# First tile in two transfers of one queue, memory tokens issued later, and new engine orders in a two-layer decoder kernel

## Chip, core and metric

The kernel runs on one core of a Trainium2 chip. The core has five engines that run side by side, each through its own list of instructions: TensorE (matmuls), VectorE, ScalarE, GpSimd and SyncE, which here only issues transfers. They wait for one another by semaphores. Data is moved by 16 DMA engines; SyncE, ScalarE and GpSimd each have a queue on which they issue transfers. The metric is the device time of one launch in microseconds, as a median over several runs.

## The reference

A decoder trunk of two layers over 256 tokens of width 1024, in 32-bit floats. Layer 0 mixes tokens by a gated unit, layer 1 by causal attention; in both, a 4-head attention into 256 memory tokens runs beside the mixer. Each layer ends in a gated feed-forward block, and every sublayer in `LayerNorm(alpha*x + f(x))`.

```
h = x @ a_w_in                       # layer 0: u (768), v (768), q_mem (256)
u = gelu(u); v = layer_norm(gelu(v), ln_g, ln_b)
mix = u * (causal(w_s) @ v + b_s)    # in chunks of 128 positions
...
h = x @ b_w_in                       # layer 1: q, k, v, q_mem
mix = softmax(q k^T / 8, causal) @ v
...
mem_out = softmax(q_mem k_mem^T / 8) @ v_mem ;  k_mem, v_mem = mem @ w_mem_kv
x = layer_norm(alpha*x + concat(mix, mem_out) @ w_mix_out)
x = layer_norm(alpha*x + (silu(x @ w_g) * (x @ w_u)) @ w_ffn_out)
```

## The kernel before

**Split operands.** Every matrix is multiplied as a high and a low part. `split` (L378) makes them: ScalarE casts the 32-bit values to the matmul's format (L379, "CAST"), VectorE subtracts the cast from the original (L380, "TENSOR_TENSOR"). Of the four products of parts the three larger ones are computed, in the order of `LO_LAST`: high x high, low tokens x high weights, high tokens x low weights.

**The weight stream.** `Stream` (L194) loads weights in units of 128 x 2048 numbers (1 MB) into four raw buffers (`RAW_BUFS`) and splits them in halves into ten buffers (`HALF_BUFS`). A raw buffer is loaded anew when both its halves have been split. The units `qm0`, `u0` and `km0` come in two transfers each (`IN_HALVES`).

**The first product.** The loop at L426 computes `va`, the values of the gated unit, and fills the stream by hand. Eight tiles (kk = 0 to 7), two to a raw buffer `raw_v`, each hold 256 columns of transposed tokens and 768 columns of weights, 512 KB. For each tile the tokens' high part is cast (L439, by VectorE for the first three tiles, then by ScalarE), their low part made (L440), the weights are split, for the first two tiles in two cuts of 384 columns, and twelve matmuls of 384 columns are issued: six with the first 384 weight columns, then six with the rest. Tile 0 comes in three transfers (L436), the others in one each (L438).

**Warm-up.** 37 small matmuls on zeros (`WARM`, L415) are issued before the first product.

**What follows it** in layer 0: the memory queries (`hqm`, weights `qm0`), `pu` (weights `u0` to `u2`), the memory keys (`hkm`) and values (`pvm`), then the gating product `sv`, which needs the normalised values `vn` (scaled at L965 and L966) and the mask-multiplied `wsT`. The memory tokens come in four transfers of 256 KB (`mraw`, L920).

**The tail.** The last token tile's output is normalised in three pieces of 512, 384 and 128 columns (`LAST_PIECES`): subtract the mean and multiply by the gain (L511), multiply by the inverse deviation and add the bias (L512), store (L514). The inverse deviation comes from L507 on VectorE and L508 on GpSimd. The last piece is stored by ScalarE's queue, the others by SyncE's.

**Order.** TensorE runs in the order in which the code issues its matmuls (`manual_schedule`). For VectorE, ScalarE and SyncE a table gives the order: `keep_order` (L358) numbers an engine's instructions as the code emits them, from 0, and chains them in the order of the table. On VectorE, 0 and 1 are two small memsets (L410, L412), 2 and 3 the high and low part of tile 0's tokens, 4 and 5 the low part of the first and the second cut of its weights, 6 to 9 the same for tile 1. On ScalarE, 0 is a table load (L400), 1 the small transfer at L425, 2 the transfer of tile 0 at L436, 3 and 4 the casts of tile 0's two cuts. On SyncE, 0 and 1 are tile 0's two transfers, 2 to 8 the other tiles, 9 and 10 the halves of `qm0`, 11 and 12 those of `u0`, 13 and 14 `u1` and `u2`, 15 and 16 the halves of `km0`, 17 the gain row, 18 to 21 the memory tokens, 22 `wsT`.

Of the kernel before, what the change touches and what calls it, by code (L numbers as in the profile page):

```python
# [22 lines left out]
D = 1024  # L23
T = 256
# [169 lines left out]
class Stream:  # L194
# [128 lines left out]
)  # L323
SCALAR_ORDER = (
# [30 lines left out]
)  # L355


# [865 lines left out]
```

## Time and profile before

| what | value |
|---|---|
| median of 3 runs | 552.55 us (552.26 to 552.84) |
| profiled execution, first to last instruction | 550.8 us |
| mean granted TensorE clock | 0.996 |
| bytes read from HBM | 119.42 MB, 219 GB/s over the span |

The profile is one execution. A row of its timeline gives start, length, engine, line, operation, output and inputs, shapes, how many instructions were merged, and in brackets how long the engine had been idle and what ended that. An engine name with a q ("SPq") is the engine's sequencer, which issues transfers. A matmul's length in the profile is from its start to the end of its pipeline, so consecutive ones overlap; the spacing of their starts is what one costs. In a row of stretches, the counts in brackets behind an engine's busy time are instructions that run in the stretch, and the last three numbers are the granted clock, the DMA engines' busy share and GB/s. Outside the span lie 1.75 us between the profiled span and the median of the runs.

### The profile page before, as it was taken

The page shows a single profiled execution, that of the slowest core. Times are in us where ns is not written, and L with a number is a line of the kernel's source. Part 1 is how long each engine was busy: PE and PEld are TensorE (multiplying, and loading weights), DVE is VectorE, ACT ScalarE, POOL GpSimd, SP SyncE. Part 2 cuts the span into 40 slices and gives each one's busy share as a digit, 9 for nine tenths or more (in the row PEclk, how much of TensorE's full clock was granted, in tenths as well). Part 3 has the DMA queues.
Part 4 walks back from the last instruction along what each step waited for, and adds up shares of the span by engine and source line. Part 5 has one row for each costly group of instructions (what it writes and reads, how often), then busy time and mean ns, then how long its engine had stood idle before and what let it go on. Part 6 is the DMA issues. An engine that isn't in the chain of part 4 may idle for free.

```text
span 550.8 us, 7698 instructions
## 1 busy us (share of the span) xinstructions
PE 542.6 (99%) x2835; PEld 460.6 (84%) x2835; DVE 501.5 (91%) x707; ACT 374.5 (68%) x574; POOL 47.7 (9%) x59
## 2 busy tenths in 40 slices
PE   9999999999999999999999999999999999999994
PEld 8988878888888888888898888788888888888884
DVE  5799978999999999999989688589999999999997
ACT  5868759785858677683565667668768676876720
POOL 1012001020202020100000000111202020201000
PEclk9999999999999999999999999999999999999998
DMA  8997668479796988878539234513597698897622
GB/s 303 384 398 265 223 259 221 154 131 328 155 343 132 300 220 229 275 271 273 198 137 397 105 130 161 114 77 153 97 360 133 249 266 271 233 255 220 218 69 77
DMA packets 23718, 120.97 MB, mean 220 GB/s; under 512 B 2688, under 2 KB 4736, under 8 KB 13824
## 3 DMA queue, kind: packets, MB, share of 16 engines
q1 hardware_dynamic: 17344, 99.16, 47.8%
q0 software_dynamic: 5760, 20.97, 21.4%
q8 instruction: 22, 0.36, 0.3%
q10 hardware_dynamic: 576, 0.34, 0.3%
q14 instruction: 16, 0.13, 0.1%
HBM read 119.42 MB, written 1.05 MB: 219 GB/s over the span
## 4 chain that ended last, share of the span: by engine, by line
PE 98%; DMA 1%; DVE 1%; DVEq 0%; ACT 0%; issue 0%
PE fof L404 11%; PE Xf L404 10%; PE Xg L404 10%; PE fog L404 9%; PE Zg L404 7%; PE Zf L404 7%; PE qk L404 6%; PE opc L404 4%; PE opa L404 4%; PE va L404 3%; PE bv L404 3%; PE pu L404 3%; PE pvm L404 3%; PE hkm L404 2%; PE hqm L404 2%; PE pg L404 2%
## 5 line engine op out<-in xcount | busy, mean ns | idle before, releaser
L379 ACT CAST spl_s_M<-raw_s_T 128x1024 fp32r<-128x1024 f32 x80 | 82.4, 1052 | 22.9 <-DVE raw_s_T L259 18.0
L380 DVE TENSOR_TENSOR spl_s_M<-raw_s_T,spl_s_M 128x1024 fp32r<-128x1024 f32 x80 | 95.6, 1217 | 2.4 <-ACT spl_s_M L379 2.1
L380 DVE TENSOR_TENSOR spl_s_M<-raw_s,spl_s_M 128x1024 fp32r<-128x1024 f32 x60 | 71.7, 1217 | 3.2 <-ACT spl_s_M L379 3.1
L379 ACT CAST spl_s_M<-raw_s 128x1024 fp32r<-128x1024 f32 x60 | 61.0, 1050 | 17.5 <-DMA raw_s<-in_w 13.3
L404 PE MATMUL fof<-spl_w,htf 128*128 128x512 f32 x264 | 63.0, 390 | 0.0
L404 PEld LDWEIGHTS fof<-spl_w,htf 128*128 128x128 f32 x264 | 49.3, 188 | 10.2
L404 PE MATMUL fog<-spl_w,htg 128*128 128x512 f32 x228 | 54.2, 390 | 0.0
L380 DVE TENSOR_TENSOR spl_w<-raw_w,spl_w 128x1024 fp32r<-128x1024 f32 x44 | 53.2, 1215 | 0.1
L404 PEld LDWEIGHTS fog<-spl_w,htg 128*128 128x128 f32 x228 | 42.7, 188 | 8.8
L259 DVE TENSOR_TENSOR raw_s_T<-raw_s_T,raw_s 128x1024 f32<-128x1024 f32 x40 | 48.4, 1217 | 0.1
L379 ACT CAST spl_w<-raw_w 128x1024 fp32r<-128x1024 f32 x44 | 45.7, 1055 | 1.0 <-PE fof L404 1.0
L404 PE MATMUL qk<-x2T,spl_qk 128*128 128x512 f32 x192 | 36.0, 343 | 0.0
L220 POOL DMA_DIRECT2D raw_s<-in_w x20 | 17.1, 856 | 217.1 <-DVE spl_s_M L380 201.4
L404 PEld LDWEIGHTS qk<-x2T,spl_qk 128*128 128x128 f32 x192 | 29.4, 188 | 4.4
L404 PE MATMUL Xg<-spl_s_M,SgM 128*128 128x512 f32 x120 | 29.4, 394 | 0.0
L404 PE MATMUL Xf<-spl_s_M,SfM 128*128 128x512 f32 x120 | 29.3, 393 | 0.0
L404 PE MATMUL Zg<-spl_s_M,SgM 128*128 128x512 f32 x120 | 28.9, 390 | 0.0
L404 PE MATMUL Xf<-spl_s_M,x1T 128*128 128x512 f32 x120 | 28.9, 390 | 0.0
L404 PE MATMUL Zf<-spl_s_M,SfM 128*128 128x512 f32 x120 | 28.8, 389 | 0.0
L404 PE MATMUL Xg<-spl_s_M,x3T 128*128 128x512 f32 x120 | 28.8, 389 | 0.0
L404 PEld LDWEIGHTS Zg<-spl_s_M,SgM 128*128 128x128 f32 x120 | 22.5, 188 | 4.8 <-DVE SgM L380 0.2
L404 PEld LDWEIGHTS Xg<-spl_s_M,x3T 128*128 128x128 f32 x120 | 22.5, 188 | 4.7
(265 smaller groups left out, 1068.8 us busy)
## 6 DMA issues: line engine op xcount, KB each, us to landing
raw_w<-in_w SPq DMA_DIRECT2D x22, 1024.0 KB, 6.6
raw_s<-in_w SPq DMA_DIRECT2D x20, 1024.0 KB, 7.1
raw_s_T<-in_w SPq DMA_DIRECT2D x10, 1024.0 KB, 7.0
raw_s_T<-in_w POOLq DMA_DIRECT2D x20, 512.0 KB, 8.6
raw_s<-in_w POOLq DMA_DIRECT2D x20, 512.0 KB, 5.5
raw_o<-in_w SPq DMA_DIRECT2D x8, 1024.0 KB, 6.4
raw_qk<-in_w SPq DMA_DIRECT2D x6, 1024.0 KB, 4.8
raw_v<-in_w SPq DMA_DIRECT2D x7, 512.0 KB, 8.1
```

Of the source, the lines that this page charges most:

```text
L220: self.nc.gpsimd.dma_start(self.raw[name][:, sl], self.unit_ap(other)[:, sl], accum_op=ALU.add)
L259: self.nc.vector.tensor_add(raw, raw, self.raw[used[1]][:, sl])
L379: nc.scalar.copy(hi, src)
L380: nc.vector.tensor_sub(lo, src, hi.bitcast(F32))
L404: nc.tensor.matmul(o, lhsT, rhs, start=start, stop=stop, skip_group_check=on)
```

## The change

Tile 0 comes in two transfers, both issued by SyncE: tokens and the first cut of the weights (640 columns, 320 KB), then the second cut (384 columns, 192 KB). ScalarE issues none of them, so it has 536 instructions instead of 537, and numbers above 2 in its table fall by one: 2 and 3 are now the casts of tile 0's two cuts, 15 the cast of tile 7's tokens, 40 to 43 those of the memory tokens. The three order tables are replaced. SyncE now issues the first memory tokens (18) behind the first half of `qm0` (9), and the next two behind the first half of `u0`. In the excerpt the tables are cut to their first and last lines.

```diff
 VECTOR_ORDER = (
-    0, 2, 3, 4, 5, 6, 7, 8, 9, 10, 11, 12, 13, 14, 16, 15, 18, 17, 19, 20, 22, 21, 23, 24, 34, 29, 33, 25, 32, 38, 37,
-    30, 27, 31, 28, 41, 46, 35, 26, 45, 49, 55, 42, 57, 47, 59, 50, 40, 1, 56, 64, 36, 58, 39, 63, 48, 95, 97, 43, 61,
...
-    661, 666, 663, 670, 664, 662, 671, 672, 673, 674, 675, 681, 676, 679, 677, 682, 680, 678,
+    0, 5, 2, 3, 4, 6, 8, 7, 9, 10, 11, 12, 14, 15, 13, 17, 16, 19, 18, 20, 21, 22, 23, 24, 33, 34, 47, 29, 25, 31, 37,
+    1, 26, 41, 42, 38, 35, 49, 46, 55, 50, 30, 36, 32, 63, 59, 39, 61, 48, 40, 56, 64, 45, 60, 27, 95, 44, 28, 57, 62,
+    51, 96, 52, 97, 58, 53, 43, 100, 54, 66, 67, 70, 74, 78, 71, 79, 69, 75, 68, 80, 73, 72, 98, 65, 81, 83, 85, 99,
...
+    669, 664, 661, 670, 671, 666, 672, 662, 673, 674, 675, 676, 677, 679, 678, 680, 681, 682,
 )
 SCALAR_ORDER = (
-    2, 3, 4, 5, 6, 7, 8, 9, 11, 10, 13, 14, 12, 15, 16, 0, 17, 1, 18, 19, 26, 27, 22, 24, 25, 31, 20, 32, 23, 41, 21,
...
+    3, 2, 4, 5, 6, 7, 8, 9, 11, 10, 13, 12, 14, 16, 40, 0, 15, 41, 17, 18, 25, 42, 22, 26, 24, 23, 21, 19, 30, 31, 35,
...
 )
 SYNC_ORDER = (
-    0, 1, 2, 3, 4, 18, 5, 6, 7, 8, 10, 9, 11, 12, 13, 14, 15, 19, 20, 16, 17, 24, 22, 25, 21, 26, 27, 28, 29, 23, 31,
...
-    113, 112, 115, 114,
+    0, 1, 2, 3, 4, 5, 6, 7, 8, 9, 18, 11, 19, 20, 10, 12, 13, 14, 21, 15, 16, 17, 24, 25, 22, 26, 27, 28, 23, 38, 29,
...
+    114, 115,
 )
...
                 if kk == 0:
-                    for q, c0, c1 in ((nc.sync, 0, T), (nc.scalar, T, T + 384), (nc.sync, T + 384, D)):
-                        q.dma_start(rk[:, c0:c1], src[:, c0:c1])
+                    for c0, c1 in ((0, T + 384), (T + 384, D)):
+                        nc.sync.dma_start(rk[:, c0:c1], src[:, c0:c1])
                 else:
                     nc.sync.dma_start(rk, src)
```

101 rows, old and new, of tables (SCALAR_ORDER, SYNC_ORDER, VECTOR_ORDER) are left out of this document.

## The prediction

> **What bounds the kernel now.** I read the shares on the page first, then what TensorE waited for, then the chain of waits over the first 60 us, which runs from the first transfer into matmuls that never stop.
>
> ```profile
> PE 542.6 (99%) x2835; PEld 460.6 (84%) x2835; DVE 501.5 (91%) x707; ACT 374.5 (68%) x574; POOL 47.7 (9%) x59
> PE warmup L415 <- DVE warm L410: 1.1, 1, 1.1
> 0.80 3.92 DMA raw_v<-in_w
> 4.72 0.02 issue
> 4.75 0.52 ACT spl_v L379
> 5.27 0.04 issue
> 5.31 17.52 PE va L404 x96
> ```
>
> The second line is all that the waits view lists for PE over the whole span: one wait, at the very start. From 5.31 us on TensorE always has its next operand in time. So the span has three parts: the way to the first real matmul (5.31 us), a matmul stream that no engine holds up, and a tail after the last matmul. The order of the matmuls is fixed by hand and the change doesn't touch it. It can therefore win only in the first and the last part; in the middle it can only lose, by making TensorE wait where it doesn't now.
>
> The stream has one soft place, its beginning. Rows of the timeline, TensorE alone, each from a narrow stretch (start, length, instructions that run in the stretch):
>
> ```profile
> 1.06 4.13 PE L415 MATMUL warmup<-warm 128*128 128x128 bf16 x37 [1.06 <-DVE warm L410]
> 5.31 1.56 PE L404 MATMUL va<-spl_v,x0T 128*128 128x384 f32 x4
> 6.71 2.60 PE L404 MATMUL va<-spl_v,x0T 128*128 128x384 f32 x14
> 7.76 5.71 PE L404 MATMUL va<-spl_v,x0T 128*128 128x384 f32 x32
> ```
>
> Later on 32 matmuls take 5.71 us; less the 0.33 us by which the last runs out, that is 5.38/31 = 0.173 us each. The fifth matmul starts at 6.71 us, so the first four took 1.40 us, 0.35 each, twice as long. The 37 warm-up matmuls of 128 columns took 0.11 us each, which is 0.33 for 384 columns: also half rate. TensorE thus runs at half rate from 1.06 to about 6.6 us, 5.5 us, whatever it does. The first four matmuls lose 1.40 - 4 x 0.173 = 0.71 us by it. That matters below: a start that comes later falls partly into time that is now spent at half rate.
>
> **The change part by part.**
>
> *The transfers of the first tile.* Before, SyncE issues tokens (128 KB) and the second half of the weights (192 KB), ScalarE the first half (192 KB).
>
> ```profile
> 0.80 0.42 ACTq L436 DMA_DIRECT2D raw_v<-in_w  x1
> 0.81 0.85 SPq L436 DMA_DIRECT2D raw_v<-in_w  x2
> 1.24 0.42 SPq L436 DMA_DIRECT2D raw_v<-in_w  x1
> raw_v<-in_w ACTq DMA_DIRECT2D x1, 192.0 KB, 3.9
> raw_v<-in_w SPq DMA_DIRECT2D x1, 192.0 KB, 4.0
> raw_v<-in_w SPq DMA_DIRECT2D x1, 128.0 KB, 3.7
> 2.00:4.00 2.00, 2.00 (x21) 2.00 (x20) 0.00 (x0) 0.53 (x1) 0.06 (x1) 1.00 0.79 187
> 4.00:6.00 2.00, 1.88 (x14) 1.61 (x12) 1.43 (x4) 1.02 (x2) 0.00 (x0) 1.00 1.05 377
> ```
>
> Issue plus time to landing: tokens 0.81 + 3.7 = 4.5, first half 0.80 + 3.9 = 4.7, second half 1.24 + 4.0 = 5.24 us. After, SyncE still issues two transfers at 0.81 and 1.24, so nothing behind them on its queue moves; ScalarE saves one issue of 0.42 us while it has nothing to do until 4.75, worth nothing. The same 512 KB (0.524 MB) must come. The last two rows end in the bytes' rate: 187 GB/s from 2 to 4 us, 377 after. If the first tile had the engines to itself, 0.374 MB would be there at 4.0 and the other 0.150 MB 0.4 us later, at 4.4. At the other end nothing changes, 5.24. For the second transfer I take 4.9, a third of the way in from the unchanged row: one queue fewer is in the way, but the next tile's transfers still crowd in from behind. The first transfer, 320 KB, lands before it and decides nothing, for the following reason.
>
> *The tables.* Number n in a table is the nth instruction of that engine as the code emits them. On VectorE 2 and 3 make the first tokens' high and low part, 4 and 5 the low part of the first and of the second half of the weights. The old table begins 0, 2, 3, 4, 5; the new one 0, 5, 2, 3, 4. On ScalarE, with the transfer gone, 2 and 3 are the casts of the first and second half; the new table begins 3, 2. Both engines are thus told to do the **second half first**, whereas the first matmuls use tokens and the first half. VectorE may not cast the tokens before it has made the low part of the second half, which needs ScalarE's cast of it, which needs the second transfer. Durations:
>
> ```profile
> 4.52 0.29 DVE L439 CAST x0T<-raw_v 128x256 fp32r<-128x256 f32 x1 [3.52 <-DMA raw_v<-in_w]
> 4.85 0.43 DVE L440 TENSOR_TENSOR x0T<-raw_v,x0T 128x256 fp32r<-128x256 f32 x1
> 5.29 1.07 DVE L380 TENSOR_TENSOR spl_v<-raw_v,spl_v 128x384 fp32r<-128x384 f32 x2
> ```
>
> From a landing at 4.90: cast of the second half 4.93 to 5.45 (0.52); its low part 5.47 to 6.00 (half of 1.07); token cast 6.01 to 6.30; first matmul 6.34 instead of 5.31. Token low part 6.34 to 6.77 (matmuls three and four need it), low part of the first half 6.78 to 7.31 (matmul five). So matmul five starts at 7.34 instead of 6.71: **+0.63 us**, if the clock has risen by about 6.6 as in this trace. In an execution where it rises before 5.3, the old kernel has its fifth matmul at 5.31 + 4 x 0.173 = 6.00 and the loss is 1.34. The three runs shown lie 0.58 us apart (552.26 to 552.84), about the size of the 0.71 that the half rate costs here, so both kinds may be among them. I take +0.85. With the landing at 4.4 the loss is at least 0.13, at 5.24 up to 1.68.
>
> *Tiles two to eight and the memory tokens.* The first memory transfer (256 KB) stood between tiles four and five and now goes out behind the first half of the memory queries' weights.
>
> ```profile
> 3.12 0.66 SPq L920 DMA_DIRECT2D mraw<-in_memT  x1
> 14.00:22.00 8.00, 8.00 (x48) 8.00 (x48) 5.55 (x9) 6.52 (x10) 0.00 (x0) 1.00 1.04 412
> 22.67 5.71 PE L404 MATMUL hqm<-x0T,spl_qm 128*128 128x512 f32 x32
> L241 SPq DMA_DIRECT2D raw_u<-in_w x2: 327/379/431, 11.9 to 12.3; - x2
> DMA to landing us min/median/max: 8.7/9.2/9.7
> 19.41 2.00 ACT L379 CAST spl_qm<-raw_qm 128x1024 fp32r<-128x1024 f32 x2 [1.00 <-DMA raw_qm<-in_w]
> 20.49 2.36 DVE L380 TENSOR_TENSOR spl_qm<-raw_qm,spl_qm 128x1024 fp32r<-128x1024 f32 x2 [0.75 <-ACT spl_qm L379]
> 16.28 1.28 ACT L400 ACT_TABLE_LOAD   x1
> ```
>
> Tiles five to eight land 256 KB / 400 GB/s = 0.65 us earlier. TensorE needs 12 x 0.173 = 2.08 us a tile and waited for none of them, so that is worth nothing. In exchange three memory transfers stand before the second half of the query weights. That half becomes the transfer that ends after 6.25 MB in units of 1024 KB, the place that the second part of raw_u has now: issued 12.3, at most 9.7 to landing, 22.0 us. ScalarE's cast (half of 2.00) and VectorE's low part (half of 2.36) end at 24.2. The query product starts at 22.67 + 0.63 = 23.3 and reaches that half after 8 of its 32 matmuls, 1.4 us, at 24.7. Cover 0.5 us; beyond that each us of lateness costs one. On ScalarE the cast of the first memory tokens and the table load (L400) now stand ahead of the eighth tile's token cast. Those memory tokens end the first 4.75 units, 4.98 MB: by the byte rates near 16 us, say 17 with the landing. Two casts (at most 1.0 each) and 1.28 later, at 20.3, the tile's tokens are there; it starts at 23.3 - 2.1 = 21.2. Cover 0.9 us.
>
> *The rest of the tables.* Both engines stay at the same instructions, only permuted. The tightest place that I find is the scaling of the gated values (instruction 58), moved to place 64, where the old order has the row that starts at 52.54.
>
> ```profile
> 52.54 0.75 DVE L470 TENSOR_TENSOR kkm<-hkm,kkm 128x256 fp32r<-128x256 f32 x2
> 51.60 1.02 DVE L966 SCALAR_TENSOR_TENSOR vn<-vn,rsv,gv 128x768 f32<-128x768 f32 x1
> 53.27 0.98 PE L404 MATMUL sv<-wsT,vn 128*64 128x128 f32 x14
> ```
>
> It would end at 52.54 + 1.02 = 53.56; TensorE wants it at 53.27 + 0.63 = 53.90. Cost nothing, bounded above by one scaling, 1.0 us. In the tail:
>
> ```profile
> 544.77 0.35 DVE L511 SCALAR_TENSOR_TENSOR xres<-xres,mvg,gb1ffn 128x128 f32<-128x128 f32 x1
> 545.04 0.15 DVE L507 TENSOR_SCALAR rsg<-mvg 128x1 f32<-128x1 f32 x1
> 545.11 1.27 DVE L511 SCALAR_TENSOR_TENSOR xres<-xres,mvg,gb1ffn 128x384 f32<-128x384 f32 x2
> 545.27 0.85 POOL L508 TENSOR_TENSOR rsg<-rsg,mhalf 128x1 f32<-128x1 f32 x1 [7.93 <-DVE rsg L507]
> 546.30 1.53 DVE L512 SCALAR_TENSOR_TENSOR xres<-xres,rsg,gb1ffn 128x128 f32<-128x128 f32 x3
> out<-xres SPq DMA_DIRECT2D x2, 256.0 KB, 2.2
> out<-xres ACTq DMA_DIRECT2D x2, 64.0 KB, 1.6
> ```
>
> The last tile keeps its six normalising steps, but the widest is no longer the last: the narrow pair is. Now VectorE ends at 546.30 + 1.53 = 547.83 and the 256 KB store behind it lands 2.2 us on, at 550.0. After: the small L507 first (544.77 to 544.84), two wide subtractions 1.2, their two scalings 1.2 (GpSimd's 0.85 is done by then), the narrow pair one behind the other 0.7: 547.9, and a 64 KB store that lands 1.6 us on, 549.5 to 549.6. **-0.4 us.**
>
> Sum: +0.85 - 0.4 = +0.45. The profiled execution (550.8) would become 551.25. The median of the runs, 552.55, is 1.75 above that span; I carry the difference over: **553.0 us**.
>
> **The rivals.**
>
> *A, the clock.* Slower. Warm-up ends at 5.19 (1.06 + 4.13) and TensorE would then idle 1.15 us instead of 0.12, just before its rate doubles. If idle time keeps the half rate, every matmul behind it costs 0.33 instead of 0.173, 48% of the time lost. Merely set back by 1.15 us, the doubling costs about 0.4; begun anew at 6.34 and lasting 5.5 us again, 2.6. I take the middle, 1.5: 554.5. For it: the half rate ended long after a seemingly full stretch of work. Against: four fifths of the time stays busy. It decides only if the gap lies before the doubling.
>
> The Trainium skill, page "TensorE: Matmul & The Clock Gate", Part 1, says that the clock is released after a window of about 3.4 us sustained activity that runs free of the kernel's start. The 5.5 us here are one window and part of another, which agrees. An estimate by that page: a window spoilt by the gap costs one more window at half rate, 3.4 x 0.48 = 1.6 us.
>
> *B, an early pair.* With one queue both parts come together, at 4.0, sooner than the byte rate above allows. Then the first matmul starts at 5.44; the fifth has its data at 6.44, but four at half rate take until 6.84. The start loses 0.13 and only the tail counts: 552.55 + 0.13 - 0.4 = 552.3; with the pair at 3.6 it would be 551.9. In this case the new order costs nothing, and the change does what its words say. Against it: 187 GB/s is the rate of all queues together.
>
> *C, a starved stream.* One of the covers (0.5 at the query weights, 0.34 at the scaling) fails and TensorE waits about 1 us: 554.0. Against: 91% busy VectorE has recovered everywhere so far.
>
> **How the numbers follow.** Forecast 0.58, A 0.22, B 0.12, C 0.08. A change of less than 0.2%, 1.1 us, can't be told from none. The forecast lies inside it, except for its late-landing end (0.07); A lies outside, C mostly; faster by 1.1 needs the second transfer at about 3.4, hardly possible (0.03). Slower 0.22 + 0.06 + 0.07 = 0.35, same 0.62. The range runs from 552.0, just under B, to 555.0, past A's middle; A begun anew is left out.
>
> **What would show it.** Right: the first va matmul near 6.3 us with VectorE's L380 ahead of L439 there; the fifth at 7.3; the same 0.173 spacing after; still no PE wait; the last transfer a 64 KB store from ScalarE. Wrong: a first matmul before 5.4; spacing of 0.33 beyond 7 us (A); a PE wait at hqm or sv (C).

## The result and the profile after

The changed kernel takes **556.36 us** (median of 6 runs, 554.30 to 558.34), the kernel before 552.75 (6 runs, 552.26 to 553.15): a ratio of 1.0069, interval 1.0051 to 1.0086. It is slower, by more than the forecast (553.0) and its range (552.0 to 555.0) allowed. The profiled execution has a span of 554.3 us, 556.03 with what lies around it.

The shares on the page have hardly moved, and TensorE is still the bound:

```profile
PE 542.7 (98%) x2835; PEld 459.6 (83%) x2835; DVE 500.4 (90%) x707; ACT 374.7 (68%) x574; POOL 50.6 (9%) x59
```

The loss is in what TensorE waits for. Before there was one wait in the whole span, now there are four (waits view, TensorE; total, times, longest):

```profile
PE Zf L404 <- ACT Zf L803: 1.7, 1, 1.7
PE va L404 <- DVE x0T L439: 1.4, 1, 1.4
PE warmup L415 <- DVE warm L410: 1.1, 1, 1.1
PE Xf L404 <- DVE spl_s_M L380: 0.6, 1, 0.6
```

To place them, take the start of the same matmul in both traces, one minus the other. That delay is +0.67 us from the sixth va matmul on, stays within 0.1 us of that until 219 us (times of the kernel before), steps to +2.59 at 219.4, to +3.49 at 234.8, to +3.83 at 236.6, and is +3.73 at the last matmul. The span grew by 3.5. So **0.7 us was lost at the start, as foreseen, 3.1 us in the middle, where the prediction had nothing**, and the tail gave back 0.2.

*The start.* The second cut in the issues of the changed kernel (KB, us to landing), then the timeline of ScalarE, VectorE and TensorE:

```profile
raw_v<-in_w SPq DMA_DIRECT2D x1, 192.0 KB, 3.8
```

```profile
5.01 0.92 ACT L379 CAST spl_v<-raw_v 128x384 fp32r<-128x384 f32 x2 [2.92 <-DMA raw_v<-in_w]
5.55 0.56 DVE L380 TENSOR_TENSOR spl_v<-raw_v,spl_v 128x384 fp32r<-128x384 f32 x1 [4.55 <-ACT spl_v L379]
6.03 0.29 DVE L439 CAST x0T<-raw_v 128x256 fp32r<-128x256 f32 x1
6.46 1.81 PE L404 MATMUL va<-spl_v,x0T 128*128 128x384 f32 x8 [1.42 <-DVE x0T L439]
```

The second cut is issued at 1.23 and lands 3.8 us later; ScalarE and VectorE work on it first, the token cast comes third, and TensorE, done with its warm-up, stands idle for 1.42 us.

*The middle.* GpSimd issues the accumulating halves of the weight units at L220. Before, then after:

```profile
198.54 0.84 POOL L220 DMA_DIRECT2D raw_s<-in_w  x1 [22.13 <-DVE spl_s_M L380]
200.14 0.87 POOL L220 DMA_DIRECT2D raw_s<-in_w  x1 [0.76 <-DVE spl_s_M L380]
201.72 0.84 POOL L220 DMA_DIRECT2D raw_s_T<-in_w  x1 [0.72 <-DVE spl_s_M L380]
```

```profile
197.89 0.85 POOL L220 DMA_DIRECT2D raw_s<-in_w  x1 [23.59 <-DVE spl_s_M L380]
199.80 0.87 POOL L220 DMA_DIRECT2D raw_s_T<-in_w  x1 [1.06 <-DVE spl_s_M L380]
201.68 0.85 POOL L220 DMA_DIRECT2D raw_s<-in_w  x1 [1.02 <-DVE spl_s_M L380]
198.12 1.23 DVE L380 TENSOR_TENSOR spl_s_M<-raw_s_T,spl_s_M 128x1024 fp32r<-128x1024 f32 x1
200.17 1.22 DVE L380 TENSOR_TENSOR spl_s_M<-raw_s,spl_s_M 128x1024 fp32r<-128x1024 f32 x1
```

Each of these loads is released by a low part on VectorE (in brackets). The last two rows are instructions 242 and 240 of VectorE's table: the old one has 240 first, the new one 242. With that, GpSimd's second load is one of `raw_s_T`, and the second half of `raw_s` goes third. ScalarE's table puts the casts of `raw_s` ahead of nearly all that follows (its timeline, before, then after):

```profile
206.43 3.90 ACT L379 CAST spl_s_M<-raw_s 128x1024 fp32r<-128x1024 f32 x4
214.50 0.59 ACT L803 COPY Zf<-m1f 128x512 f32<-128x512 f32 x1
```

```profile
211.81 2.95 ACT L379 CAST spl_s_M<-raw_s 128x1024 fp32r<-128x1024 f32 x3 [5.37 <-DMA raw_s<-in_w]
221.31 0.59 ACT L803 COPY Zf<-m1f 128x512 f32<-128x512 f32 x1
221.94 2.34 PE L404 MATMUL Zf<-spl_s_M,x1T 128*128 128x512 f32 x9 [1.68 <-ACT Zf L803]
```

ScalarE, 68% busy over the span, stands for 5.37 us behind one late transfer, is then busy without a break for ten microseconds, and its copy at L803 comes 6.8 us later than before. TensorE starts 10.21 us behind the landing of that load (at 211.73). The other wait, 0.6 us at 238, is for a low part on VectorE (264 in the table, moved from place 262 to 270, behind gain rows of L547 that were pulled forward).

*The tail.* The narrow pair is last and a 64 KB store ends the program, as predicted:

```profile
550.95 0.35 DVE L511 SCALAR_TENSOR_TENSOR xres<-xres,mvg,gb1ffn 128x128 f32<-128x128 f32 x1
551.33 0.35 DVE L512 SCALAR_TENSOR_TENSOR xres<-xres,rsg,gb1ffn 128x128 f32<-128x128 f32 x1
551.72 0.34 ACTq L514 DMA_DIRECT2D out<-xres  x1
```

### The profile page after: what moved, and what is told of

It is laid out like the page before. It is cut to its first block, busy times and chain, and to the rows that moved or that the text cites. A ratio compares the mean times of both kernels' runs of the same rounds, so it can differ in the third digit from the quotient of the medians.

```text
span 554.3 us, 7703 instructions
## 1 busy us (share of the span) xinstructions
PE 542.7 (98%) x2835; PEld 459.6 (83%) x2835; DVE 500.4 (90%) x707; ACT 374.7 (68%) x574; POOL 50.6 (9%) x59
## 3 DMA queue, kind: packets, MB, share of 16 engines
q0 software_dynamic: 5760, 20.97, 21.1%
## 4 chain that ended last, share of the span: by engine, by line
PE 92%; DVE 4%; issue 2%; DMA 1%; ACT 1%; POOLq 0%; POOL 0%; SPq 0%; DVEq 0%
PE Xg L404 10%; PE fof L404 10%; PE fog L404 9%; PE Xf L404 9%; PE Zg L404 7%; PE qk L404 6%; PE Zf L404 6%; PE opc L404 4%; PE opa L404 4%; PE va L404 3%; PE bv L404 3%; PE pu L404 3%; PE pvm L404 3%; PE hkm L404 2%; PE hqm L404 2%; PE pg L404 2%
## 5 line engine op out<-in xcount | busy, mean ns | idle before, releaser
L380 DVE TENSOR_TENSOR spl_s_M<-raw_s_T,spl_s_M 128x1024 fp32r<-128x1024 f32 x80 | 95.9, 1218 | 2.5 <-ACT spl_s_M L379 2.2
L380 DVE TENSOR_TENSOR spl_s_M<-raw_s,spl_s_M 128x1024 fp32r<-128x1024 f32 x60 | 72.0, 1218 | 3.5 <-ACT spl_s_M L379 3.5
L380 DVE TENSOR_TENSOR spl_w<-raw_w,spl_w 128x1024 fp32r<-128x1024 f32 x44 | 53.0, 1217 | 1.8 <-ACT spl_w L379 1.7
L220 POOL DMA_DIRECT2D raw_s<-in_w x20 | 17.1, 857 | 214.9 <-DVE spl_s_M L380 211.4
L220 POOL DMA_DIRECT2D raw_s_T<-in_w x20 | 17.4, 880 | 139.2 <-DVE spl_s_M L380 119.5
L404 PEld LDWEIGHTS Zf<-spl_s_M,SfM 128*128 128x128 f32 x120 | 22.4, 188 | 5.1 <-ACT m5f L769 0.5
```

Source lines behind the costliest of these rows:

```text
L220: self.nc.gpsimd.dma_start(self.raw[name][:, sl], self.unit_ap(other)[:, sl], accum_op=ALU.add)
L380: nc.vector.tensor_sub(lo, src, hi.bitcast(F32))
L404: nc.tensor.matmul(o, lhsT, rhs, start=start, stop=stop, skip_group_check=on)
```

## The experiments

The theory after the result is that the tables lose the time, at two places, the start's reversed order and the exchange of 240 and 242, and that the clock (rival A) adds something. The rivals are that the transfers do it, that the clock does it alone, or that other parts of the tables cost as much. In the diffs NEW and OLD stand for the tables of the changed kernel and of the kernel before, cut as in Python and written out in the kernels; OLD is renumbered where ScalarE has one instruction less. The kernel before ran beside each on the same chip: 552.65 us (29 runs) for the first four below; 552.70 (17) for the exchange of 240 and 242, the move of 264, the repaired start with the old middle, and the longer warm-up alone; 552.73 (32) for the two repairs, the longer warm-up with the exchange, the tail, and the early places; 553.04 (15) for the last two. Each ratio is against these.

**Transfers or tables.** First the new transfers with the old tables, then the old transfers with the new tables.

```diff
-VECTOR_ORDER, SCALAR_ORDER, SYNC_ORDER = NEW_V, NEW_S, NEW_Y
+VECTOR_ORDER, SCALAR_ORDER, SYNC_ORDER = OLD_V, OLD_S, OLD_Y
```

> The two new transfers of tile 0 with the three old tables (ScalarE's without the removed issue); the memory tokens are back in their early place with the old SyncE table. Theory (all loss comes from the tables): first va matmul within 0.3 us of 5.31, no TensorE wait over 0.2 us later on, median 552.3 to 552.9. Rival (the transfers bring the loss, by crowding or by semaphores): over 554.

Measured: 553.05 us, ratio 1.0003 (0.9994 to 1.0013), no wait of TensorE but the first. Its first matmul starts at 4.97 instead of 5.31:

```profile
4.97 3.34 PE L404 MATMUL va<-spl_v,x0T 128*128 128x384 f32 x15
```

```diff
-                    for c0, c1 in ((0, T + 384), (T + 384, D)):
-                        nc.sync.dma_start(rk[:, c0:c1], src[:, c0:c1])
+                    for q, c0, c1 in ((nc.sync, 0, T), (nc.scalar, T, T + 384), (nc.sync, T + 384, D)):
+                        q.dma_start(rk[:, c0:c1], src[:, c0:c1])
```

> The kernel before with the three new tables; tile 0 in three transfers as before. Theory (tables alone): as slow as the changed kernel or a few tenths slower, 556 to 557.5, first va matmul near 6.7 us, waits of TensorE between 200 and 245 us. Rival (transfers): near 553.

Measured: 556.15 us, ratio 1.0057 (1.0035 to 1.0078), as slow as the change within its interval. The tables lose the time; two transfers instead of three are worth nothing that can be measured. This trace has something else, which the section on the clock takes up.

**The start alone.** The first cut goes first again.

```diff
 VECTOR_ORDER = (
-    0, 5, 2, 3, 4, 6, 8, 7, 9, 10, 11, 12, 14, 15, 13, 17, 16, 19, 18, 20, 21, 22, 23, 24, 33, 34, 47, 29, 25, 31, 37,
+    0, 2, 3, 4, 5, 6, 8, 7, 9, 10, 11, 12, 14, 15, 13, 17, 16, 19, 18, 20, 21, 22, 23, 24, 33, 34, 47, 29, 25, 31, 37,
...
 SCALAR_ORDER = (
-    3, 2, 4, 5, 6, 7, 8, 9, 11, 10, 13, 12, 14, 16, 40, 0, 15, 41, 17, 18, 25, 42, 22, 26, 24, 23, 21, 19, 30, 31, 35,
+    2, 3, 4, 5, 6, 7, 8, 9, 11, 10, 13, 12, 14, 16, 40, 0, 15, 41, 17, 18, 25, 42, 22, 26, 24, 23, 21, 19, 30, 31, 35,
```

> The changed kernel, but tile 0's first half goes first again on VectorE (0, 2, 3, 4, 5) and ScalarE (2, 3); all else as changed. Theory (the start's loss comes from the order of the halves alone): first va matmul near 5.2 us instead of 6.46, end of the va product 0.7 to 1.2 us earlier, and the later waits of TensorE (Zf, Xf near 220 to 240 us) still there, so a median some 0.8 us under the changed kernel's 556.4 and still a wide spread of the runs. Rival (the single queue delivers tile 0 late): first va matmul stays after 6 us.

Measured: 554.56 us (12 runs), ratio 1.0030 (1.0019 to 1.0040), 1.8 us under the changed kernel. The first matmul starts at 5.12, and the delay behind it is -0.68 us. But the second tile then comes too late, its casts keep TensorE waiting at 8.24 (0.75 us) and 9.17 (0.31), and the delay is +0.71, as in the changed kernel: in this trace the gain is gone at once. That its last matmul is still 1.75 us ahead of the changed kernel's comes from elsewhere: there is no wait at 222. The third load on GpSimd's queue, the second half of `raw_s`, is issued at 201.92 here and lands at 210.03, 8.1 us later, against 10.05 us in the changed kernel's trace. In the five traces with the new order at that place the same load takes 8.1, 8.5, 8.65, 10.05 and 10.3 us, and TensorE then starts late by 0, 0.2, 0.2, 1.8 and 2.3 us at 222. In the four of them in which it waits, it starts 10.21 or 10.22 us behind that load's landing; in the ten traces of other kernels that have the old order there, it starts 12.0 us or more behind the landing of that half. So the order makes that wait possible, and the load's time in the execution makes its size.

**The middle.** First the old order for a long stretch, then single exchanges.

```diff
-VECTOR_ORDER, SCALAR_ORDER, SYNC_ORDER = NEW_V, NEW_S, NEW_Y
+VECTOR_ORDER = NEW_V[:183] + OLD_V[183:331] + NEW_V[331:]
+SCALAR_ORDER = NEW_S[:186] + OLD_S[186:288] + NEW_S[288:]
+SYNC_ORDER = NEW_Y[:51] + OLD_Y[51:72] + NEW_Y[72:]
```

> The changed kernel with the old order in one middle stretch: VectorE places 183 to 330, ScalarE 186 to 287, SyncE 51 to 71 (about 150 to 300 us). Theory (the wait at 222 us is made by the new order of that stretch): TensorE waits only at the start, span about 551.3, median 553.0 to 553.4, spread of the runs about as before's. Rival (the loss sits in several places, or comes from transfers late in any order): over 554.5.

Measured: 555.56 us, ratio 1.0042 (1.0029 to 1.0056). The waits at 222 and 238 are gone, but the gain is only 0.8 us, which the interval doesn't separate from nothing; the theory's 553.0 to 553.4 is missed, and the rival's median fits. A new wait of 0.4 us for L803 stands at 160 us. There VectorE already runs the old order (from 142 us) and ScalarE still the new one (until about 174), so that wait may come from the join, and this run alone doesn't tell what the middle costs.

```diff
 VECTOR_ORDER = (
...
-    232, 235, 237, 220, 236, 230, 239, 223, 242, 229, 240, 238, 255, 243, 233, 245, 244, 246, 253, 247, 250, 249, 241,
+    232, 235, 237, 220, 236, 230, 239, 223, 240, 229, 242, 238, 255, 243, 233, 245, 244, 246, 253, 247, 250, 249, 241,
```

> The changed kernel with instructions 240 and 242 of VectorE's table exchanged, so that the gated sum's low part (242) stands behind the third weight piece (240) as before. Theory (order of the two weight streams on GpSimd's queue): the accumulating loads go out raw_s, raw_s, raw_s_T, raw_s_T again, the second raw_s half lands near 207 instead of 211.7, ScalarE's idle stretch of 5.4 us before it goes, and TensorE's wait at 222 (1.84 us, Zf for ScalarE's L803) is gone; the wait at 238 (Xf for VectorE's spl_s_M) may stay. Median 554.5 to 555.5 against 556.4. Rival (the whole stretch is late because VectorE is short of time there): the wait at 222 stays above 1 us and the median stays within 0.4 of 556.4.

Measured: 554.80 us, ratio 1.0040 (1.0027 to 1.0052): 1.56 us under the changed kernel by **one exchange in a table of 683**. With six runs of each the two intervals just touch, so the size is uncertain; the argument rests on the traces. GpSimd's queue and ScalarE's idle time in its trace:

```profile
199.81 0.84 POOL L220 DMA_DIRECT2D raw_s<-in_w  x1 [23.94 <-DVE spl_s_M L380]
201.69 0.87 POOL L220 DMA_DIRECT2D raw_s<-in_w  x1 [1.04 <-DVE spl_s_M L380]
203.83 0.85 POOL L220 DMA_DIRECT2D raw_s_T<-in_w  x1 [1.27 <-DVE spl_s_M L380]
209.63 2.96 ACT L379 CAST spl_s_M<-raw_s 128x1024 fp32r<-128x1024 f32 x3 [1.43 <-DMA raw_s<-in_w]
```

The two `raw_s` loads are neighbours again, the second lands at 209.55 (not near 207, as expected, but 2.2 us sooner than in the changed kernel), ScalarE waits 1.43 us instead of 5.37, and TensorE waits neither at 222 nor at 238 (the four traces with the new order there and 264 in its place all have the second, 0.4 to 0.6 us by the waits view). By the delay that second place costs more than its wait, 1.0 to 1.4 us between 234 and 237 us in those four traces, also where nothing was lost at 222; in the ten traces of other kernels with the old order the delay doesn't grow there. The second wait was thus a consequence of the first order too, although the low part 264 stands where it stood. To test that from the other side, 264 alone was moved forward:

```diff
 VECTOR_ORDER = (
...
-    256, 254, 234, 252, 260, 259, 265, 248, 263, 291, 287, 258, 266, 251, 267, 268, 257, 283, 271, 264, 292, 261, 293,
+    256, 254, 234, 252, 260, 259, 265, 248, 263, 291, 287, 258, 266, 264, 251, 267, 268, 257, 283, 271, 292, 261, 293,
```

> The changed kernel with instruction 264 of VectorE's table alone (low part of a raw_s_T half) moved from place 270 to just behind 266, ahead of the gain rows. Theory (the pulled-forward gain rows make it late): the waits of TensorE at 238 and 240 (Xf for VectorE's spl_s_M, 0.96 us together) shrink below 0.3; the wait at 222 stays; median about 1 us under 556.4, 555.2 to 555.8. Rival (that low part is late because its load is): the wait at 238 stays above 0.7 and the median stays at 556.4 within 0.4.

Measured: 557.80 us (5 runs), ratio 1.0102 (1.0085 to 1.0118): a miss. The wait for `spl_s_M` is gone, as the theory had it, but the median is 1.4 us above the changed kernel's, not 1 us under it. In its trace, 3.27 us behind the changed kernel's at the last matmul, 1.7 us come before 219 us (the clock rises late, at 10.1 us), 0.5 from a longer wait at 222 (2.16 us for L803; the load took 10.3 us) and 1.6 from the clock, which falls behind that wait, as shown below; the place at 235 costs 0.5 less. That run, 559.3, is one of two near 559.5; the other three lie at 557.6 to 557.8, and why they are above the changed kernel's median no trace shows.

**Both repairs**, the start's and the exchange of 240 and 242; then the start's with the old middle from an earlier place on.

```diff
-    0, 5, 2, 3, 4, 6, 8, 7, 9, 10, 11, 12, 14, 15, 13, 17, 16, 19, 18, 20, 21, 22, 23, 24, 33, 34, 47, 29, 25, 31, 37,
+    0, 2, 3, 4, 5, 6, 8, 7, 9, 10, 11, 12, 14, 15, 13, 17, 16, 19, 18, 20, 21, 22, 23, 24, 33, 34, 47, 29, 25, 31, 37,
...
-    232, 235, 237, 220, 236, 230, 239, 223, 242, 229, 240, 238, 255, 243, 233, 245, 244, 246, 253, 247, 250, 249, 241,
+    232, 235, 237, 220, 236, 230, 239, 223, 240, 229, 242, 238, 255, 243, 233, 245, 244, 246, 253, 247, 250, 249, 241,
...
-    3, 2, 4, 5, 6, 7, 8, 9, 11, 10, 13, 12, 14, 16, 40, 0, 15, 41, 17, 18, 25, 42, 22, 26, 24, 23, 21, 19, 30, 31, 35,
+    2, 3, 4, 5, 6, 7, 8, 9, 11, 10, 13, 12, 14, 16, 40, 0, 15, 41, 17, 18, 25, 42, 22, 26, 24, 23, 21, 19, 30, 31, 35,
```

> The changed kernel with two repairs of some entries each: first half of the first tile's weights done first on ScalarE and VectorE, and VectorE's 240 and 242 exchanged. All other places are those of the changed kernel. Theory (these two places hold the loss): first va near 5.1 us, no wait above 0.3 us between 200 and 245, median 552.8 to 553.5, as with the old middle (553.44). Rival (the rest of the new middle costs as well, by the 0.6 to 0.9 us wait at 238): median 554 or more.

Measured: 553.66 us (11 runs), ratio 1.0020 (1.0011 to 1.0029), just above the range of the theory and well under that of the rival. No wait is left behind 10 us. What is left lies at the second tile:

```profile
5.42 2.39 PE L404 MATMUL va<-spl_v,x0T 128*128 128x384 f32 x12 [0.53 <-ACT spl_v L379]
8.60 0.62 PE L404 MATMUL va<-spl_v,x0T 128*128 128x384 f32 x2 [0.79 <-ACT spl_v L379]
9.52 0.80 PE L404 MATMUL va<-spl_v,x0T 128*128 128x384 f32 x3 [0.31 <-DVE x0T L440]
```

```diff
-VECTOR_ORDER, SCALAR_ORDER, SYNC_ORDER = NEW_V, NEW_S, NEW_Y
+VECTOR_ORDER = NEW_V[:1] + OLD_V[1:5] + NEW_V[5:159] + OLD_V[159:331] + NEW_V[331:]
+SCALAR_ORDER = OLD_S[:2] + NEW_S[2:131] + OLD_S[131:288] + NEW_S[288:]
+SYNC_ORDER = NEW_Y[:43] + OLD_Y[43:72] + NEW_Y[72:]
```

> The changed kernel with the first half of the first tile's weights done first on ScalarE and VectorE, and the old tables from place 159 to 330 (VectorE), 131 to 287 (ScalarE), 43 to 71 (SyncE). What stays new: the transfers, the memory tokens behind the first tiles, the later places, the tail. Theory (start and middle hold the loss): first va near 5.1, no wait at 219 to 240, median 552.6 to 553.6, within 0.2% of the kernel before. Rival (the early places with the memory tokens cost too, by a late tile 1 or a wait near 160): median 554 or more, with PE waits before 20 us or at 150 to 165.

Measured: 553.44 us (11 runs), ratio 1.0013 (1.0004 to 1.0021), with the same two waits near 8.4 and 9.3 us. These are waits that the rival expected; the median is the theory's. So the two repairs do as much as the repaired start with the long old stretch, within the runs' spread. Start and middle hold 2.7 to 2.9 of the 3.6 us.

**The clock.** In the trace with the old transfers and the new tables, TensorE's first matmuls, then rows of one microsecond each (TensorE's busy time and matmuls first; granted clock, DMA share and GB/s last):

```profile
6.77 1.19 PE L404 MATMUL va<-spl_v,x0T 128*128 128x384 f32 x4 [2.10 <-DVE x0T L439]
7.00:8.00 1.00, 1.00 (x5) 0.73 (x5) 0.84 (x3) 0.39 (x1) 0.00 (x0) 0.69 1.01 414
8.00:9.00 1.00, 1.00 (x4) 1.00 (x4) 0.85 (x3) 0.65 (x3) 0.00 (x0) 0.50 1.08 324
9.00:10.00 1.00, 1.00 (x4) 1.00 (x4) 0.96 (x4) 0.72 (x1) 0.00 (x0) 0.50 0.96 295
10.00:11.00 1.00, 1.00 (x5) 1.00 (x5) 1.00 (x2) 0.83 (x2) 0.00 (x0) 0.60 1.02 365
11.00:12.00 1.00, 1.00 (x8) 1.00 (x7) 0.70 (x2) 0.37 (x2) 0.00 (x0) 1.00 0.98 389
```

The clock was up, falls to half at 7.38 (0.38 at 1 and 0.62 at 0.5 make the 0.69) and rises at 10.8: 3.4 us. Behind TensorE's idle gap of 2.10 us four matmuls fit in a microsecond, not eight, and the delay grows from 1.00 to 2.37 us. With 240 and 242 exchanged the clock rises only at 9.8 us. There the column reads 1.00 throughout (it does so ahead of a trace's first change), and the counts of matmuls tell it:

```profile
7.00:8.00 1.00, 1.00 (x4) 1.00 1.13 406
8.00:9.00 1.00, 1.00 (x4) 1.00 0.90 291
9.00:10.00 1.00, 1.00 (x5) 1.00 1.02 320
10.00:11.00 1.00, 1.00 (x8) 1.00 1.03 352
```

The delay is 2.14 us there behind 8 us, against 0.84 in the trace with the old middle, whose first matmul starts at the same 6.63 us with the clock up. So rival A exists, in both of its forms, at 1.3 to 1.4 us each. Of the five traces with the late first matmul and 37 warm-up matmuls, three have it and two (the changed kernel's, where the clock was up from 4.74, and the one with the old middle) don't. Two kernels with more warm-up matmuls are meant to measure its share:

```diff
-WARM = 37
+WARM = 47
```

> The changed kernel with 47 warm-up matmuls instead of 37, which keep TensorE busy until about 6.3 us, just before its first real matmul. Theory (the idle gap costs only where the clock falls again, in some executions): median 0.2 to 0.8 below 556.4 and the largest times fewer. Rival A of the prediction (the gap keeps the half rate in most executions): median 1.0 to 1.6 below, 554.8 to 555.4. No share for the clock: median within 0.2 of 556.4.

Measured: 555.74 us (6 runs, 555.43 to 556.30), ratio 1.0054 (1.0042 to 1.0066): 0.6 us under the changed kernel, as the theory had it, and a spread of 0.9 instead of 4.0 us. The two intervals overlap, so the medians alone can't tell it from nothing.

```diff
-WARM = 37
+WARM = 47
...
-    232, 235, 237, 220, 236, 230, 239, 223, 242, 229, 240, 238, 255, 243, 233, 245, 244, 246, 253, 247, 250, 249, 241,
+    232, 235, 237, 220, 236, 230, 239, 223, 240, 229, 242, 238, 255, 243, 233, 245, 244, 246, 253, 247, 250, 249, 241,
```

> The changed kernel with instructions 240 and 242 exchanged and 47 warm-up matmuls: no wait left at 222 and no idle gap before the first real matmul, but the first matmul still late. Theory (the share of the clock in the changed kernel's loss is about 0.6 to 1.0 us, spread over the executions): the rate doubles before 7.3 us and stays; median 553.7 to 554.3 against 554.8 with the exchange alone, spread under 1 us. Rival (the clock matters only in the executions whose profile was taken): median 554.6 to 555.0.

Measured: 553.64 us (11 runs, 552.81 to 555.12), ratio 1.0021 (1.0012 to 1.0030): 1.16 us under the same kernel with 37. The largest of these runs stay a microsecond and a half above the median; the spread expected under 1 us is 2.3. The longer warm-up fills the gap only where the rate is still half: in this trace the clock rose at 3.87, the 47 were done at 5.18, and TensorE idled 1.61 us all the same. By these two the clock's share is some 0.6 to 1.2 us of the median, and the runs don't fix it closer.

**The tail.**

```diff
-VECTOR_ORDER, SYNC_ORDER = OLD_V, OLD_Y
+VECTOR_ORDER, SYNC_ORDER = OLD_V[:654] + NEW_V[654:], OLD_Y[:110] + NEW_Y[110:]
```

> The kernel before with the new tables' last part alone: VectorE from place 654, SyncE from place 110 (the last two token tiles' normalising and stores). The prediction had -0.4 us for the tail, the changed kernel's trace shows -0.2 against its last matmul. Theory: the last store lands 0.15 to 0.3 us sooner behind the last matmul than before, median 552.3 to 552.6, which its interval can't tell from the kernel before. Rival (the tail gives nothing or costs): median 552.7 or more.

Measured: 552.53 us (11 runs) against 552.73, ratio 0.9996 (0.9987 to 1.0005). In its trace the end comes 7.00 us behind the start of the last matmul, before 7.23. The sign is the predicted one and the size about half. The median can't be told from nothing, but the traces agree: the end comes 6.99 to 7.07 us behind the start of the last matmul in all twelve with the new tail, 7.23 to 7.30 in all four with the old one.

**The early transfers.** The new early places with everything else old, then SyncE's part of them alone, then the two repairs with the first memory transfer back at its old place.

```diff
-VECTOR_ORDER, SCALAR_ORDER, SYNC_ORDER = NEW_V, NEW_S, NEW_Y
+VECTOR_ORDER = OLD_V[:5] + NEW_V[5:117] + OLD_V[117:]
+SCALAR_ORDER = OLD_S[:2] + NEW_S[2:82] + OLD_S[82:]
+SYNC_ORDER = OLD_Y[:5] + NEW_Y[5:38] + OLD_Y[38:]
```

> The changed kernel with the old tables, except VectorE's places 5 to 116, ScalarE's 2 to 81 and SyncE's 5 to 37, which are the new ones: the memory tokens behind the first tiles and what goes with it, with the first half of the first tile's weights done first. Theory (these places cost nothing, as the prediction had it): 553.05, as with the old tables throughout, within 0.3 us; TensorE waits for nothing between 20 and 60 us. Rival (the memory tokens' place makes tile two late, by the waits of 0.3 to 0.9 us near 8 us that the runs with the early places showed): median 553.4 to 554.0 and such a wait in the trace.

Measured: 554.17 us (11 runs), ratio 1.0021 (1.0012 to 1.0030), 1.1 us more than with the old tables throughout. The trace has waits of 0.3 us twice near 8 us, as the rival had it, and one of 0.2 us at 97, 12 us behind the place where VectorE goes over to the old table. The theory falls: the early places cost something.

```diff
-VECTOR_ORDER, SCALAR_ORDER, SYNC_ORDER = NEW_V, NEW_S, NEW_Y
+VECTOR_ORDER, SCALAR_ORDER = OLD_V, OLD_S
+SYNC_ORDER = OLD_Y[:5] + NEW_Y[5:38] + OLD_Y[38:]
```

> The changed kernel with the old tables on VectorE and ScalarE, and of SyncE's table the new places 5 to 37 alone: only the order of the early transfers changes, first of all the first memory transfer, sixth before and eleventh now. Theory (this order makes the second tile late): its weights and tokens land after 7.4 us instead of 6.8, TensorE waits 0.3 to 1 us near 8 to 9 us, median 553.6 to 554.2 against 553.05 with the old tables throughout. Rival (the late second tile comes with the early order on VectorE or ScalarE, or by chance): it lands before 7.2, no wait near 8 us, median within 0.3 of 553.05.

Measured: 557.50 us (4 runs), ratio 1.0084 (1.0070 to 1.0098). The second tile lands at 7.10 us and nothing waits near 8: the theory falls, and the rival's median is missed too. The time is lost later, in waits that neither SyncE's new order with the new tables nor the old order with the old ones has, so the mixture seems to make them. Its largest waits stand at 67 to 72 us, and one stands where the prediction had a cover of 0.5 us, at the second half of the query weights (VectorE's timeline):

```profile
23.70 1.23 DVE L380 TENSOR_TENSOR spl_qm<-raw_qm,spl_qm 128x1024 fp32r<-128x1024 f32 x1 [2.89 <-ACT spl_qm L379]
```

Its low part begins 2.89 us after VectorE was free for it, and TensorE's `hqm` waits 0.8 us for it.

```diff
 SYNC_ORDER = (
-    0, 1, 2, 3, 4, 5, 6, 7, 8, 9, 18, 11, 19, 20, 10, 12, 13, 14, 21, 15, 16, 17, 24, 25, 22, 26, 27, 28, 23, 38, 29,
+    0, 1, 2, 3, 4, 18, 5, 6, 7, 8, 9, 11, 19, 20, 10, 12, 13, 14, 21, 15, 16, 17, 24, 25, 22, 26, 27, 28, 23, 38, 29,
```

> The kernel with the two repairs, and the first memory transfer back at its old place, sixth on SyncE. Theory (its move makes the second tile late): that tile lands before 7.2 us, the waits of 0.95 and 0.47 us at 8.6 and 9.5 us go, median 552.7 to 553.2. Rival (its place doesn't matter): the waits stay, the median stays at 553.66 within 0.3.

Measured: 553.42 us (11 runs), ratio 1.0011 (1.0002 to 1.0020), not to be told from the 553.66 without the move. The second tile lands at 7.59, not before 7.2. One wait of 0.3 us stands at it (at 9.11), another at a later tile (13.85); the wait of 0.79 us is gone, but the clock rose only at 7.00 in this trace, so TensorE came to the tile later. The landing and the median speak for the rival: the place of the first memory transfer does not make the second tile late by itself.

No kernel of these beats the kernel before.

## Why the prediction was wrong

**What bounds the kernel** was right, and so was what follows from it: the change can win only at the two ends, and in the middle it can only lose.

**The first tile** came out as worked: second cut at 5.0 (4.9 predicted), first matmul at 6.46 (6.34), the fifth at 7.30 (7.34), VectorE's L380 ahead of L439. The trace's delay, +0.59 us at the fifth and +0.67 from the sixth on, is the +0.63 of the clock's late rise. In the median the start is worth more than the 0.85 taken: putting the first cut first gains 1.8 us alone and 1.1 on top of the exchange of 240 and 242. More warm-up on top of the exchange gains as much, 1.16, with the first matmul as late as ever. So what the repaired start gains there is no more than what a longer warm-up gains, probably by the clock.

**The step that failed** is "Both engines stay at the same instructions, only permuted. The tightest place that I find is the scaling of the gated values [...] Cost nothing, bounded above by one scaling, 1.0 us." The scaling did cost nothing; there is no wait at sv. But the search went by the slack of VectorE's instructions against TensorE. The exchange of 240 and 242 costs VectorE nothing either. What it does is to release GpSimd's loads in another order; through them ScalarE stood 5.37 us, and ScalarE has the copy that TensorE needs. The prediction had looked at queues for the early transfers only, and at none for the 600 places behind. In place of nothing it cost 1.8 us at 219 and 1.2 us at 235 in the profiled execution. By the one exchange it is 1.56 us of the median, or 0.9 on top of the repaired start.

**Rival A** was given 0.22 as one case among others. The traces show it in three of five executions with the late start, at 1.3 to 1.4 us, near the 1.5 taken. It was not an alternative to the forecast but an addition to it. One condition, "It decides only if the gap lies before the doubling", was wrong: in the first trace above the clock fell *after* it had risen. The Trainium skill, "TensorE: Matmul & The Clock Gate", Part 1, has the rule of a free-running window of 3.41 us; the stretch at half rate from 7.38 to 10.8 us agrees with it.

**Rival C**, a starved stream, is what happened, at another place and at three times the price. The covers it named (query weights, scaling) held in the changed kernel. The cover of 0.5 us at the query weights was a thin one: with the other engines' order left old it was overrun by 0.8 us. **Rival B** didn't occur; the pair did not come early. Yet the start that it took for granted, without a loss, is what the old tables show: 553.05, nothing gained.

**The tail** was worth 0.2, not 0.4 us. The 2.2 us were the median of the two 256 KB stores; the one that ends the kernel before landed 2.0 us behind its issue, against 1.6 for the new last store. And that one is issued 4.45 us behind the start of the last matmul, 0.13 later than the old one. The shift from span to median, 1.75 us, was 1.73 in the profiled execution.

Of the 3.6 us in the medians the two repairs together take back 2.7, less than the 1.8 and 1.56 that each takes alone add up to. The waits at the second tile in both traces with the repaired start would explain that: an earlier TensorE runs into that tile, which is late. That tile goes with the remaining 0.7 to 0.9 us. **Why it is late stays open.** Its landing differs from trace to trace, 6.76 to 8.34 us. It was at most 7.14 in all four traces with the old early order on VectorE and ScalarE, and above 7.14 in eleven of the twelve others; but nothing that those two tables put in another order runs before that tile's transfer is issued at 1.70, and moving SyncE's later transfers did not decide it. It goes with the DMA engines' rate: between 4 and 6 us they moved 361 to 377 GB/s in the six traces in which it landed by 7.16, and 266 to 315 in eight of the ten others. Open too is why the same load on GpSimd's queue takes 8.1 us in one execution and 10.3 in another.

## What to carry to other kernels

In a new order, look for what each instruction releases as well as for what it needs: list the queues that an engine's ends feed, and compare the order of the loads on them, over the whole program and not only around the edit. A gap on TensorE near its start costs up to its own length and, in part of the executions, 3.4 us at half rate on top; treat that as a sum with a chance and not as a rival. Where a median differs from its forecast and the profiled execution doesn't show it, look at other traces of the same start before inventing a cause.

## What was not expected of the hardware

The clock falls for less than a whole idle window. In the trace with 264 moved, TensorE waits 2.16 us at 222 in the middle of a dense stream, and the granted clock behind it (TensorE alone, two microseconds each):

```profile
222.00:224.00 2.00, 0.00 (x0) 1.00 0.00 0
224.00:226.00 2.00, 1.86 (x6) 0.79 0.82 223
226.00:228.00 2.00, 2.00 (x6) 0.50 0.98 371
228.00:230.00 2.00, 2.00 (x9) 0.86 0.95 393
```

0.79 and 0.86 put the fall at 225.2 and the rise at 228.6. The Trainium skill, "TensorE: Matmul & The Clock Gate", under "HAM oscillation", warns of idle gaps over about 3.4 us; here gaps of 2.10 and 2.16 us were enough, and the measurement decides. A gap of 1.42 us (changed kernel) and one of 1.61 (the last kernel with 47 warm-up matmuls) left the clock up. What tells the four apart in these traces is TensorE's busy share, by the profile's modelled ends, of the 3.41 us that hold the gap, counted in steps of 3.41 us from the rise: 0.39 and 0.37 where the clock fell, 0.58 and 0.53 where it stayed. A late transfer of half a megabyte can so cost a wait and then, for 3.4 us, half of TensorE's rate.

The accumulating loads on GpSimd's queue keep the DMA engines busy twice as long for a byte as the plain ones. The changed kernel's queues on the page (packets, MB, share of 16 engines), then the two queues that are busy between 208 and 210 us, and that stretch of its windows:

```profile
q1 hardware_dynamic: 17344, 99.36, 47.1%
q0 software_dynamic: 5760, 20.97, 21.1%
q0 software_dynamic: 118, 0.42, 106.7%
q8 instruction: 1, 0.02, 3.0%
```

```profile
208.00:210.00 2.00, 2.00 (x11) 1.65 (x10) 2.00 (x3) 0.00 (x0) 0.00 (x0) 1.00 1.10 219
```

GpSimd's 40 loads of 512 KB are the 20.97 MB of q0: 1.0% of the engines' time a MB, against 0.47 on q1. From 208 to 210 us, with no plain load among them, the engines are full (1.10) at 219 GB/s; with plain loads alone they carried 414 at a share of 1.01, between 7 and 8 us in the first trace of the section on the clock. The late half of `raw_s` landed at 206.66 as the second load on that queue, before, and at 211.73 as the third, after.
